# Halving the loads of a 2x upsampling kernel: eight loads with two 8 KiB descriptors per partition in place of four with one of 32 KiB

## The chip, the cores and the metric

The kernel runs on one core of a Trainium2 chip. The metric is the device time of one execution in microseconds (us). The 16 DMA engines of the core move data between DRAM and the on-chip memory SBUF (128 partitions). VectorE (DVE) and ScalarE (ACT) copy inside SBUF. SyncE (SP) only issues DMAs. A *descriptor* is one contiguous piece that one DMA engine moves. Each load or store here is split over all 16 engines, eight partitions each, and each engine works through its pieces in the order in which they were issued. I call that queue of one engine its *ring*.

## The reference

Nearest-neighbour upsampling by 2: each element of x, float32 [16, 64, 64, 64] (16.78 MB), is written to a 2 x 2 square of the output (67.11 MB). No arithmetic is involved.

```python
for i in range(new_h):
    for j in range(new_w):
        result[:, :, i, j] = x[:, :, i // scale_factor, j // scale_factor].copy()
```

## The kernel before

All rows of x are seen as one list of 65,536 rows of 64 numbers (256 bytes). There are four loads (NB = 4) of 4 MiB. Partition p gets 128 consecutive rows: one descriptor of 32 KiB. All four are issued at once, at the start, into buffers of their own. Then, for each of 16 tiles (32 rows per partition), DVE expands rows 0 to 17 and ACT rows 18 to 31 into `u` (32 KiB per partition, two buffers), and SP stores `u` as one 4 MiB DMA.

```python
K, J = 32, 4
NB = R // (P * J * K)
xf = x.rearrange("b c h w -> (b c h) w").rearrange(
    "(n p r) w -> n p r w", n=NB, p=P
)
of = out.rearrange("b c (h hd) w -> (b c h) (hd w)", hd=s).rearrange(
    "(n p r) w -> n p r w", n=NB, p=P
)
KV = 18
xpool = ctx.enter_context(tc.tile_pool(name="xin", bufs=NB))
upool = ctx.enter_context(tc.tile_pool(name="uexp", bufs=2))
xts = []
for n in range(NB):
    xt = xpool.tile([P, J * K, W], fdt, name="xt")
    nc.sync.dma_start(out=xt[:, :, :], in_=xf[n])
    xts.append(xt)
# ... expanded(): a broadcast view that repeats each row and each column twice
for n in range(NB):
    for j in range(J):
        r0 = j * K
        u = upool.tile([P, K, s, W, s], fdt, name="u")
        nc.vector.tensor_copy(out=u[:, :KV], in_=expanded(xts[n][:, r0 : r0 + KV, :]))
        nc.scalar.copy(out=u[:, KV:], in_=expanded(xts[n][:, r0 + KV : r0 + K, :]))
        nc.sync.dma_start(out=of[n, :, r0 : r0 + K, :], in_=u[:, :, :, :, :])
```

(Lines joined; the first load is also moved ahead of the start barrier, which the change leaves alone.)

Of the kernel before, what the change touches and what calls it, by code (L numbers as in the profile page):

```python
# [1 line left out]

# [4 lines left out]


def begin_before_barrier(nc):



    blocks = nc.main_func.blocks
    main, body = blocks[0], blocks[1]
    sp = mybir.EngineType.SP
    load = next(i for i in body.instructions if i.engine == sp)
    assert isinstance(load, mybir.InstDMACopy), type(load)
    assert not (load.sync_info and load.sync_info.on_wait)
    body.instructions = [i for i in body.instructions if i is not load]
    kept = list(main.instructions)  # L20
    at = next(
        n
        for n, i in enumerate(kept)
        if i.engine == sp and isinstance(i, mybir.InstDrain)
    )
    kept.insert(at, load)
    main.instructions = kept


@with_exitstack  # L30
def kernel(
    ctx: ExitStack,
    tc: tile.TileContext,
    x: bass.AP,
    scale_factor: int,
    out: bass.AP,
):
    nc = tc.nc
    nc.at_finalize(begin_before_barrier)
    P = nc.NUM_PARTITIONS  # L40
    s = int(scale_factor)
    B, C, H, W = x.shape
    R = B * C * H
    fdt = x.dtype




    K, J = 32, 4
    NB = R // (P * J * K)  # L50
    assert NB * P * J * K == R
    xf = x.rearrange("b c h w -> (b c h) w").rearrange(
        "(n p r) w -> n p r w", n=NB, p=P
    )
    of = out.rearrange("b c (h hd) w -> (b c h) (hd w)", hd=s).rearrange(
        "(n p r) w -> n p r w", n=NB, p=P
    )

    KV = 18

    xpool = ctx.enter_context(tc.tile_pool(name="xin", bufs=NB))
    upool = ctx.enter_context(tc.tile_pool(name="uexp", bufs=2))

    xts = []
    for n in range(NB):
        xt = xpool.tile([P, J * K, W], fdt, name="xt")
        nc.sync.dma_start(out=xt[:, :, :], in_=xf[n])
        xts.append(xt)

    def expanded(rows):  # L70
        k = rows.shape[1]
        return rows.unsqueeze(2).unsqueeze(4).to_broadcast([P, k, s, W, s])

    for n in range(NB):
        for j in range(J):
            r0 = j * K
            u = upool.tile([P, K, s, W, s], fdt, name="u")
            nc.vector.tensor_copy(  # L78
                out=u[:, :KV], in_=expanded(xts[n][:, r0 : r0 + KV, :])
            )  # L80
            nc.scalar.copy(  # L81
                out=u[:, KV:], in_=expanded(xts[n][:, r0 + KV : r0 + K, :])
            )
            nc.sync.dma_start(
                out=of[n, :, r0 : r0 + K, :], in_=u[:, :, :, :, :]
            )


# [1 line left out]
_INS = ['x', 'scale_factor']  # L90
_OUTS = [((16, 64, 128, 128), 'float32')]

_NUMBERS = {'scale_factor': 2}


# [26 lines left out]
```

## Time and profile before

The time is 199.99 us (median of 3; 199.96 to 200.03).

| what | value | where it is read |
|---|---|---|
| span of the profiled run | 198.2 us | page |
| DMA: bytes, mean rate | 83.89 MB, 423 GB/s | page |
| busy DVE / ACT | 21% / 26% | page |
| one store, steady state | 9.68 us | distance of copies in the timeline |

The page of the kernel before: busy time by engine (us, share of the span, instructions), the DMA row (busy tenths in 40 slices), the packets and the one DMA queue.

```profile
DVE 40.9 (21%) x16; ACT 52.0 (26%) x17; POOL 0.2 (0%) x4
...
DMA  8999999999999999999999999999999999999994
...
DMA packets 2880, 83.89 MB, mean 423 GB/s; under 512 B 320, under 2 KB 320, under 8 KB 320
...
q1 hardware_dynamic: 2880, 83.89, 98.8%
```

The compute engines are idle about three quarters of the time and the DMA engines hardly ever (98.8% busy): the kernel is bound by what they move. There are 2560 data packets and 320 small completion writes.

The timeline of the kernel before (start, duration, engine, line, what, and in brackets the idle time ahead of it and what ended it):

```profile
0.00 2.15 SPq L67 DMA_DIRECT2D xt<-in_x_dram  x4
...
12.35 6.26 ACT L81 COPY u<-xt 128x3584 f32<-128x3584 f32 x2 [10.28 <-DMA xt<-in_x_dram]
...
15.55 165.91 SPq L84 DMA_DIRECT2D out_dram<-u  x16
52.07 3.18 ACT L81 COPY u<-xt 128x3584 f32<-128x3584 f32 x1 [33.47 <-DMA out_dram<-u]
...
61.75 3.18 ACT L81 COPY u<-xt 128x3584 f32<-128x3584 f32 x1 [6.51 <-DMA out_dram<-u]
...
71.43 3.18 ACT L81 COPY u<-xt 128x3584 f32<-128x3584 f32 x1 [6.49 <-DMA out_dram<-u]
```

The third copy of ACT needs the `u` buffer of the first store back, so its start, 52.07, tells when the first store landed. That store was issued near 15.6 us, but it lay behind four loads in the rings. After that a copy starts every 9.68 us: one 4.19 MB store each, 433 GB/s. The 3.2 us copies are hidden, as the other store moves meanwhile.

### The profile page before, as it was taken

The page shows a single profiled execution, that of the slowest core. Times are in us where ns is not written, and L with a number is a line of the kernel's source. Part 1 is how long each engine was busy: PE and PEld are TensorE (multiplying, and loading weights), DVE is VectorE, ACT ScalarE, POOL GpSimd, SP SyncE. Part 2 cuts the span into 40 slices and gives each one's busy share as a digit, 9 for nine tenths or more (in the row PEclk, how much of TensorE's full clock was granted, in tenths as well). Part 3 has the DMA queues.
Part 4 walks back from the last instruction along what each step waited for, and adds up shares of the span by engine and source line. Part 5 has one row for each costly group of instructions (what it writes and reads, how often), then busy time and mean ns, then how long its engine had stood idle before and what let it go on. Part 6 is the DMA issues. An engine that isn't in the chain of part 4 may idle for free.

```text
span 198.2 us, 145 instructions
## 1 busy us (share of the span) xinstructions
DVE 40.9 (21%) x16; ACT 52.0 (26%) x17; POOL 0.2 (0%) x4
## 2 busy tenths in 40 slices
DVE  0055000000405050505050505050505050404000
ACT  2057000000415150606060606060606060505000
POOL 0000000000000000000000000000000000000000
DMA  8999999999999999999999999999999999999994
GB/s 317 423 423 430 450 430 456 370 403 423 423 423 436 436 443 456 436 436 423 423 423 423 423 443 443 450 450 436 423 423 423 423 423 436 436 443 456 436 436 212
DMA packets 2880, 83.89 MB, mean 423 GB/s; under 512 B 320, under 2 KB 320, under 8 KB 320
## 3 DMA queue, kind: packets, MB, share of 16 engines
q1 hardware_dynamic: 2880, 83.89, 98.8%
HBM read 16.78 MB, written 67.11 MB: 423 GB/s over the span
## 4 chain that ended last, share of the span: by engine, by line
DMA 77%; ACT 14%; issue 0%; ACTq 0%
DMA out_dram<-u 70%; ACT u L81 14%; DMA xt<-in_x_dram 6%; ACTq L81 0%
## 5 line engine op out<-in xcount | busy, mean ns | idle before, releaser
L81 ACT COPY u<-xt 128x3584 f32<-128x3584 f32 x16 | 50.8, 3179 | 128.3 <-DMA out_dram<-u 118.0
L78 DVE COPY u<-xt 128x4608 f32<-128x4608 f32 x16 | 40.9, 2560 | 139.6 <-DMA out_dram<-u 127.3
L81 ACT ACT_TABLE_LOAD x1 | 1.3, 1283 | 0.8 <-PEq L103 0.8
L103 POOL MEMSET const-bfloat16-1.0<- 128x1 bf16 x1 | 0.1, 102 | 0.0
L103 POOL MEMSET const-uint8-127<- 128x1 uint8 x1 | 0.1, 102 | 0.0
L103 POOL MEMSET const-float32-0.0<- 128x1 f32 x1 | 0.1, 99 | 0.2 <-issue 0.2
L103 POOL MEMSET const-float32-1.0<- 128x1 f32 x1 | 0.1, 99 | 0.0
## 6 DMA issues: line engine op xcount, KB each, us to landing
out_dram<-u SPq DMA_DIRECT2D x16, 4096.0 KB, 16.1
xt<-in_x_dram SPq DMA_DIRECT2D x4, 4096.0 KB, 25.9
```

Source lines behind the costliest of these rows:

```text
L78: nc.vector.tensor_copy(out=u[:, :KV], in_=expanded(xts[n][:, r0 : r0 + KV, :]))
L81: nc.scalar.copy(out=u[:, KV:], in_=expanded(xts[n][:, r0 + KV : r0 + K, :]))
L103: nc = _bacc.Bacc("TRN2", target_bir_lowering=False, num_devices=1)
```

## The change

The intent is a finer start: a first load of half the size, so that the first tiles can be expanded earlier, while each tile's store becomes one contiguous 4 MiB block of the output.

```diff
-    K, J = 32, 4
-    NB = R // (P * J * K)
-    xf = ... "(n p r) w -> n p r w", n=NB, p=P
-    of = ... "(n p r) w -> n p r w", n=NB, p=P
+    K, J = 32, 2
+    rows = P * K
+    NL = R // (J * rows)
+    xf = x.rearrange("b c h w -> (b c h) w").rearrange(
+        "(n j p k) w -> n p j (k w)", n=NL, j=J, p=P
+    )
+    of = out.rearrange("b c (h hd) w -> (b c h) (hd w)", hd=s)
...
-        xt = xpool.tile([P, J * K, W], fdt, name="xt")
-        nc.sync.dma_start(out=xt[:, :, :], in_=xf[n])
+        xt = xpool.tile([P, J, K, W], fdt, name="xt")
+        nc.sync.dma_start(out=xt[:, :, :, :], in_=xf[n])
...
-            nc.sync.dma_start(
-                out=of[n, :, r0 : r0 + K, :], in_=u[:, :, :, :, :]
-            )
+        nc.sync.dma_start(
+            out=of[t * rows : (t + 1) * rows, :], in_=u[:, :, :, :, :]
+        )
```

(Cut: assertions, pool sizes and the loop over tiles, now `for t in range(NL * J)` with `xt, j = xts[t // J], t % J`.) The loads are now eight of 2 MiB. Per partition each brings two 8 KiB pieces that lie 1 MiB apart in DRAM.

More of the change, by code (lines that the diff above doesn't have):

```diff
@@ L44, with expanded @@
     fdt = x.dtype
-    K, J = 32, 4
-    NB = R // (P * J * K)
-    assert NB * P * J * K == R
+    K, J = 32, 2
+    rows = P * K
+    NL = R // (J * rows)
+    assert NL * J * rows == R
+    KV = 18
     xf = x.rearrange("b c h w -> (b c h) w").rearrange(
-        "(n p r) w -> n p r w", n=NB, p=P
+        "(n j p k) w -> n p j (k w)", n=NL, j=J, p=P
     )
-    of = out.rearrange("b c (h hd) w -> (b c h) (hd w)", hd=s).rearrange(
-        "(n p r) w -> n p r w", n=NB, p=P
-    )
-    KV = 18
-    xpool = ctx.enter_context(tc.tile_pool(name="xin", bufs=NB))
+    of = out.rearrange("b c (h hd) w -> (b c h) (hd w)", hd=s)
+    xpool = ctx.enter_context(tc.tile_pool(name="xin", bufs=NL))
     upool = ctx.enter_context(tc.tile_pool(name="uexp", bufs=2))
     xts = []
-    for n in range(NB):
-        xt = xpool.tile([P, J * K, W], fdt, name="xt")
-        nc.sync.dma_start(out=xt[:, :, :], in_=xf[n])
+    for n in range(NL):
+        xt = xpool.tile([P, J, K, W], fdt, name="xt")
+        nc.sync.dma_start(out=xt[:, :, :, :], in_=xf[n])
         xts.append(xt)
-    def expanded(rows):
-        k = rows.shape[1]
-        return rows.unsqueeze(2).unsqueeze(4).to_broadcast([P, k, s, W, s])
-    for n in range(NB):
-        for j in range(J):
-            r0 = j * K
-            u = upool.tile([P, K, s, W, s], fdt, name="u")
-            nc.vector.tensor_copy(
-                out=u[:, :KV], in_=expanded(xts[n][:, r0 : r0 + KV, :])
-            )
-            nc.scalar.copy(
-                out=u[:, KV:], in_=expanded(xts[n][:, r0 + KV : r0 + K, :])
-            )
-            nc.sync.dma_start(
-                out=of[n, :, r0 : r0 + K, :], in_=u[:, :, :, :, :]
-            )
+    def expanded(part):
+        return part.unsqueeze(2).unsqueeze(4).to_broadcast(
+            [P, part.shape[1], s, W, s]
+        )
+    for t in range(NL * J):
+        xt, j = xts[t // J], t % J
+        u = upool.tile([P, K, s, W, s], fdt, name="u")
+        nc.vector.tensor_copy(out=u[:, :KV], in_=expanded(xt[:, j, :KV, :]))
+        nc.scalar.copy(out=u[:, KV:], in_=expanded(xt[:, j, KV:, :]))
+        nc.sync.dma_start(
+            out=of[t * rows : (t + 1) * rows, :], in_=u[:, :, :, :, :]
+        )
 _INS = ['x', 'scale_factor']
```

## The prediction

> **What bounds the kernel now.** The 16 DMA engines, from start to end. The page's DMA line gives 83.89 MB at a mean of 423 GB/s and one queue that fills 98.8% of the 16 engines' span of 198.2 us; VectorE is busy 21% and ScalarE 26%. The chain of waits is load, then stores; the 3.2 us copies between are hidden by the other buffer's store. In the timeline, copies of the steady state start every 9.68 us (71.43, 81.10, 90.79, ...): one 4.19 MB store per 9.68 us, 433 GB/s. The Trainium skill, "DMA: Bandwidth & Descriptors", section "Where 436 GB/s comes from", gives a ceiling of 435 GB/s for the fabric; this trace is within 1% of it. The trace's completion times: the four loads land at 12.3, 22.0, 31.8 and 42.3 us (9.7 us apart, 10.5 for the last), the first store at 52.0, the others 9.68 us apart.
>
> So about 0.85 us is lost where loads turn into stores.
>
> **What the change does.** Bytes, copies (16 + 16, same shapes), stores (16 x 4 MB) and buffers stay. The first load is half as large, so its data should arrive near 7.5 us instead of 12.3 us, and the first two copies and the first store are issued some 5 us earlier. But all loads are issued in the first 3 to 5 us, ahead of every store, into the same rings: the first store still waits behind 16.78 MB of loads. Gain on the critical path: none. The instruction order also shows that store k of the first eight now waits for load k (shared semaphores); load 1 lands near 12.5 us, still 30 us before the rings run out of loads. No cost.
>
> A store's destination becomes one contiguous 4 MB block instead of 32 KiB pieces 128 KiB apart. Stores already run at 433 GB/s, so I expect nothing there (9.68 us per store stays).
>
> Load descriptors shrink from 32 KiB (32 per engine) to 8 KiB (128 per engine): 96 more per engine, plus 4 more completion writes. The same page, section "Why small descriptors are slow (HBM only)", names a fixed overhead of about 3 cycles per packet: 96 x 3.5 ns = 0.34 us, an estimate. From the trace: 9.68 us / 8 = 1.210 us per 32 KiB descriptor against 1.205 us at the ceiling, so up to 5 ns each, 0.5 us. Alternating between places 1 MiB apart might cost more. I expect the eight loads to land 4.9 us apart, the last near 42.8 us (42.3 before): +0.3 to +1 us, all on the critical path since nothing hides it.
>
> **Prediction:** 200.5 us, 8 in 10 between 199.6 and 202.0. Faster by over 2%: 0.01; within 2%: 0.94; slower by over 2%: 0.05.
>
> **What would show it right or wrong.** Right: first copy starts near 7.5 us; the third copy (first store landed) starts at 52.1 to 53 us, against 52.07; then every 9.68 us; DMA share still near 99%; packets 4480 instead of 2880. Wrong: a store period other than 9.68 us (the contiguous destination matters); loads landing over 5.1 us apart (8 KiB descriptors or the 1 MiB stride cost more); a gap in DMA at 5 to 20 us (the sequencer or the rings can't take eight loads in advance); a different loss where loads turn into stores.
>
> **What would make it wrong.** An 8 KiB read costing 25 ns or more of overhead (96 x 25 = 2.4 us) would put the time above the range. To be 2% faster it would have to beat the 435 GB/s ceiling, which I exclude.

## The result, and the profile after

The time is 199.85 us (median of 4; 199.79 to 199.88), against 200.01 us before (median of 4; 199.96 to 200.46). The ratio is 0.9987, with a 95% interval of 0.9969 to 1.0004: the same within noise. (A ratio here is the mean time of one kernel's fast runs over that of the other's in the same rounds, so not quite the ratio of the medians that I quote.)

The page of the changed kernel, the same lines as before:

```profile
DVE 40.9 (21%) x16; ACT 52.1 (26%) x17; POOL 0.2 (0%) x4
...
DMA  7999999999999999999999999999999999999995
...
DMA packets 4480, 83.89 MB, mean 424 GB/s; under 512 B 384, under 2 KB 384, under 8 KB 384
...
q1 hardware_dynamic: 4480, 83.89, 99.2%
```

The timeline of the changed kernel:

```profile
0.00 13.59 SPq L66 DMA_DIRECT2D xt<-in_x_dram  x8
...
7.67 6.26 ACT L78 COPY u<-xt 128x3584 f32<-128x3584 f32 x2 [5.55 <-DMA xt<-in_x_dram]
...
13.72 167.81 SPq L79 DMA_DIRECT2D out_dram<-u  x16
52.31 3.18 ACT L78 COPY u<-xt 128x3584 f32<-128x3584 f32 x1 [38.38 <-DMA out_dram<-u]
...
61.91 3.18 ACT L78 COPY u<-xt 128x3584 f32<-128x3584 f32 x1 [6.42 <-DMA out_dram<-u]
...
71.57 3.18 ACT L78 COPY u<-xt 128x3584 f32<-128x3584 f32 x1 [6.48 <-DMA out_dram<-u]
```

The first copy starts 4.7 us earlier (7.67 against 12.35), but the first store lands 0.24 us later (52.31 against 52.07). The early start only lengthened ACT's wait for the `u` buffer, from 33.47 to 38.38 us. The eight loads took SP 13.6 us to issue instead of 2 us for four: it was held up, and so the first store was issued only 1.8 us earlier (13.72 against 15.55). That costs nothing here, as the DMA row shows no gap.

The same total hides two differences that nearly cancel. The trace's completion times (16 per DMA, one from each engine; the last is taken) show them. Distances in us:

```
                                   before                 after
loads, 4 MiB each / 2 MiB each     9.70 9.71 10.53        4.96 4.97 4.98 4.97 4.97 4.97 4.96
last load -> first store           9.70                   9.73
stores after that (mean of 15)     9.68                   9.67
```

(1) The changed loads are slower while they run: 2 x 4.97 = 9.94 us per 4 MiB against 9.71. Over four times 4 MiB that is +0.9 us. (2) In the kernel before, the last load takes 0.83 us longer than its fellows; in the changed kernel it does not. I call this the *loss at the turn* from loads to stores. The packets of one engine around it, as the trace records them (start on the trace's own clock, which is 11.05 us ahead of the timeline's before and 11.26 us after; duration, ns). The trace does not name the engine: packets are joined where one starts within a few ns of the end of another.

```
before   49.03 load 1946 | 50.97 load 1653 | 52.63 store 1213 | 53.84 store 1213   (32 KiB each)
after    51.62 load  321 | 51.94 load  309 | ... | 52.87 store 1224 | 54.09 store 1213   (loads 8 KiB)
```

In the kernel before, the last load packet of every engine takes 1.65 to 2.07 us and the one ahead of it up to 1.95 us (1213 ns each until then), and the first store behind them is at full speed at once. The windows view shows the same as rates. Kernel before, its stretch of full-speed loads and the 4 us at the turn (columns: stretch, length, busy DVE, ACT, POOL, clock, DMA share, GB/s; a packet is counted whole where it starts, so short stretches are coarse, as shares over 1 show: 16 packets of 32 KiB more or less are 131 GB/s in 4 us):

```profile
14.00:38.00 24.00, 3.38 (x2) 4.61 (x2) 0.00 (x0) 1.00 1.00 430
38.00:42.00 4.00, 0.00 (x0) 0.00 (x0) 0.00 (x0) 1.00 1.09 377
```

The changed kernel:

```profile
14.00:38.00 24.00, 0.00 (x0) 0.00 (x0) 0.00 (x0) 1.00 1.01 422
38.00:42.00 4.00, 0.00 (x0) 0.00 (x0) 0.00 (x0) 1.00 1.19 500
```

While loads run, 430 against 422 GB/s; at the turn, 377 against 500, which tells the direction but not the size; the landings above give that.

So two questions are left for experiments. Why are the loads slower: descriptor size (theory D, one fixed cost per descriptor), or the places 1 MiB apart (theory A)? And why did the loss at the turn go: descriptor size again (D), the contiguous destination of the stores (theory S), the stores queued behind the loads (theory Q), or is it a fixed price of the loads' end (theory F)?

### The profile page after: what moved, and what is told of

The parts are those of the page before. It is cut to its first block, busy times and chain, and to the rows that moved or that the text cites. A ratio compares the mean times of both kernels' runs of the same rounds, so it can differ in the third digit from the quotient of the medians.

```text
span 198.0 us, 149 instructions
## 1 busy us (share of the span) xinstructions
DVE 40.9 (21%) x16; ACT 52.1 (26%) x17; POOL 0.2 (0%) x4
## 4 chain that ended last, share of the span: by engine, by line
DMA 76%; ACT 14%; issue 0%; ACTq 0%; SPq 0%
DMA out_dram<-u 73%; ACT u L78 14%; DMA xt<-in_x_dram 4%; ACTq L78 0%; SPq L79 0%
```

## The experiments

Twelve kernels ran. Times in us, with the kernel before run on the same chip in the same rounds. "Loss" is how much longer the last load took than the pace of those before it, from completion times.

| run | loads per engine | pace per 4 MiB | loss at the turn | time | ratio to before, 95% |
|---|---|---|---|---|---|
| before | 32 x 32 KiB | 9.71 | 0.83 | 199.99 | |
| changed | 128 x 8 KiB | 9.94 | none | 199.85 | 0.9969 to 1.0004 |
| e1_pad8k | 128 x 8 KiB, adjacent | 9.87 | none | 200.07 | 0.9990 to 1.0017 |
| e2_strided_store | 128 x 8 KiB | 9.94 | none | 200.01 | 0.9986 to 1.0011 |
| e3_one_tile | 128 x 8 KiB, 1 MiB loads | 9.94 | none (0.04) | 199.68 | 0.9972 to 0.9997 |
| e4_taper | 24 x 32, 8 x 24, 8 x 8 KiB | 9.71 | 0.8 | 199.95 | 0.9985 to 1.0010 |
| e5_last_first | 32 x 32 KiB, no store queued | 9.70 | none (0.01) | 204.51 | one run |
| e6_first_store_8k | 32 x 32 KiB | 9.71 | 0.95 | 200.04 | 0.9987 to 1.0018 |
| e7_2k | 512 x 2 KiB | 10.84 | none | 205.01 | one run |
| e8_16k | 64 x 16 KiB | 9.78 | 0.18 | 199.85 | 0.9978 to 1.0003 |
| f1_last_8k | 24 x 32, then 32 x 8 KiB | 9.71, 9.96 | 0.49 | 199.73 | 0.9970 to 0.9995 |
| f2_last_32k | 96 x 8, then 8 x 32 KiB | 9.94 | 0.22 | 199.69 | 0.9963 to 0.9996 |
| f3_gate_half | 24 x 32, 16 x 16 KiB, store late | 9.71 | none | 199.95 | 0.9979 to 1.0006 |
| f4_gate_3_8 | 24 x 32, 8 x 12, 8 x 20 KiB, store late | 9.72 | none | 199.44 | 0.9955 to 0.9980 |

(For f2, the loss is the 9.93 us of its last load less 9.71, the pace of 32 KiB descriptors.) "None" means within 0.05 us of zero or below it. The median of before was 200.04 (e1 to e4), 199.96 (e5 to e8), 200.09 (f1, f3, f4) and 199.94 (f2).

Totals that differ by 0.3 us or less need care. The traces show that the program ends 0.81 to 1.06 us after its last store has landed, and this tail differs between the kernels: 1.06 us in before, e1 and e5, 1.00 in e4, f2, f3 and f4, 0.88 in e6 and f1, 0.81 in the changed kernel, e2, e3, e7 and e8. In the kernel before SP still works through five semaphore waits there, some 0.06 us each, in the changed kernel through one.

### e1_pad8k: only the descriptor size

```diff
 # kernel before
-        xt = xpool.tile([P, J * K, W], fdt, name="xt")
-        nc.sync.dma_start(out=xt[:, :, :], in_=xf[n])
+        xt = xpool.tile([P, J, K * W + 16], fdt, name="xt")
+        nc.sync.dma_start(
+            out=xt[:, :, : K * W],
+            in_=xf[n].rearrange("p (j k) w -> p j (k w)", j=J),
+        )
```

> The kernel before with one thing changed: each SBUF tile is padded by 64 bytes after every 8 KiB, so each of the four loads is made of four 8 KiB descriptors per partition instead of one of 32 KiB, from the same consecutive addresses. Theory D (descriptor size does both things seen): loads land 9.9 us apart instead of 9.7, the extra 0.8 us of the last load goes (under 0.3 us is left), the time is within 0.3 us of the changed kernel (199.85 us). Theory A (the places 1 MiB apart make the loads slower): loads stay 9.7 us apart. Theory S (the contiguous destination of the stores removes the loss at the turn): the last load still lands 10.5 us after the one before it.

The loads landed 9.88, 9.87 and 9.85 us apart: theory D for both differences. Descriptor size alone slows the loads by 0.16 us per 4 MiB and removes the loss, with the stores' addresses untouched. The 0.07 us per 4 MiB that this falls short of the changed kernel's 9.94 may belong to the places apart or to the finer loads; e3 speaks for the latter. The time is not lower because its first load landed 0.56 us later (first copy at 12.91 us against 12.35), together with a longer issue of the four-piece pattern (0.70 against 0.40 us, medians).

### e2_strided_store: only the stores' addresses

```diff
 # changed kernel; wrong output on purpose
-    of = out.rearrange("b c (h hd) w -> (b c h) (hd w)", hd=s)
+    of = out.rearrange("b c (h hd) w -> (b c h) (hd w)", hd=s).rearrange(
+        "(n p q k) w -> n q p (k w)", n=NL * J // 4, p=P, q=4
+    )
-            out=of[t * rows : (t + 1) * rows, :], in_=u[:, :, :, :, :]
+            out=of[t // 4, t % 4], in_=u[:, :, :, :, :]
```

> The changed kernel, with the stores at the addresses of the kernel before (32 KiB pieces 128 KiB apart; the output is wrong on purpose). Theory D: same as the changed kernel within 0.1 us, last load 4.97 us after the one before it. Theory S: the loss of about 0.8 us at the turn from loads to stores comes back, 200.6 us.

Theory S falls: with the old addresses the last load still takes 4.96 us, no loss. The stores average 9.69 us here against 9.67 in the changed kernel: 15 x 0.02 = 0.3 us, too little for these runs to prove. The time is 0.16 us above the changed kernel's, where 0.1 was expected. The Trainium skill, "DMA: Bandwidth & Descriptors", section "Latency and other measured facts", reports slow copies between DRAM tensors at large power-of-two row pitches (2 MiB and up) and close to the full rate at 512 KiB. The pitch here is 128 KiB, and the trace agrees in that it costs nearly nothing (9.69 against 9.67 us per store).

### e3_one_tile: no places 1 MiB apart

```diff
 # changed kernel
-    K, J = 32, 2
+    K, J = 32, 1
```

> The changed kernel with sixteen loads of one tile: still 8 KiB descriptors, but each load reads one contiguous 1 MiB, without places 1 MiB apart. Theory D: 4 MiB of loads take 9.9 us or a little more (twice as many completions), time within 0.2 us of the changed kernel. Theory A: loads return to 9.7 us per 4 MiB, time about 199.0 us.

Sixteen loads land 2.486 us apart on average: 9.94 us per 4 MiB, as in the changed kernel. Theory A falls: contiguous loads are no faster. The time, 199.68, is within the 0.2 us of the changed kernel that theory D gave.

### e7_2k: the cost per descriptor at 2 KiB

```diff
 # changed kernel; wrong output on purpose
-        "(n j p k) w -> n p j (k w)", n=NL, j=J, p=P
+        "(n j p k) w -> n p j (k w)", n=NL, j=4 * J, p=P
...
+            out=xt.rearrange("p j (c k) w -> p (j c) (k w)", c=4), in_=xf[n]
```

> The changed kernel with loads of 2 KiB descriptors (512 per engine instead of 128; wrong output on purpose). A fixed cost per descriptor of 9 ns (from 9.94 against 9.70 us per 4 MiB for 24 descriptors more per engine) gives 0.0835 us each, 42.8 us for all loads, the last landing at about 45.4 us, 203 us in all. [...]

The loads landed 5.42 us apart, 84.7 ns per 2 KiB descriptor: near the 83.5 expected. With it, the average times of four sizes lie on one line. From 2 and 32 KiB: (1213.4 - 84.7) / 30 = 37.6 ns per KiB, and 84.7 - 2 x 37.6 = 9.4 ns fixed.

| descriptor | measured, ns (completion writes included) | 9.4 + 37.6 per KiB |
|---|---|---|
| 32 KiB (before) | 1213.4 | from it |
| 16 KiB (e8) | 611.5 | 611.4 |
| 8 KiB (changed; e1) | 310.5; 308.5 | 310.4 |
| 2 KiB (e7) | 84.7 | from it |

96 descriptors more per engine x 9.4 ns = 0.90 us: the whole of (1).

This cost is an average over a run, and not one constant. Counted packet by packet (16 packets in order of their starts are one per engine), the traces show two stretches. In the changed kernel an engine takes 306.4 ns per 8 KiB descriptor for about its first 40 loads, and 310.6 ns from about 16 us on. The same step comes in e2, e3, f2 and, smaller and later, e1 (306.0, then 308.2); e7 goes from 80 or 81 ns to 84.7 at about 12 us. The early times (1210.1, 608, 306.4 and 81 ns for 32, 16, 8 and 2 KiB) lie close to a line of their own, about 5 ns + 37.65 per KiB; the fixed part roughly doubles later. What doubles it is not shown. Queued stores are not needed for it: in e3 it has come by 18 us, and the first store is issued at 24.84.

The total missed, 205.0 instead of 203: the first load landed at 9.8 us, 4.4 us above its pace of 5.4, where the changed kernel has 2.7 (7.67 less 4.97). One load took SP 5.3 us to issue (median), so here the start and the issue cost too.

### e8_16k: half way

```diff
 # kernel before
-    K, J = 32, 4
+    K, J = 32, 2
```

> The kernel before with eight loads of 2 MiB and one contiguous 16 KiB descriptor per partition. A fixed cost per descriptor: 4 MiB of loads take 9.75 to 9.8 us. The loss at the turn, if it goes with the descriptor size: about 0.4 us; if it is there or not there: 0.8 or 0. Time 199.5 to 200.1 us.

The pace is on the line. The loss is 0.18 us: neither proportional to the descriptor size (0.4) nor there-or-not-there.

### e4_taper: small descriptors only just ahead of the turn

```diff
 # kernel before
-        nc.sync.dma_start(out=xt[:, :, :], in_=xf[n])
+        cut = J * K if n < NB - 1 else (J - 1) * K
+        nc.sync.dma_start(out=xt[:, :cut, :], in_=xf[n, :, :cut, :])
+        if cut < J * K:
+            nc.sync.dma_start(out=xt[:, cut:, :], in_=xf[n, :, cut:, :])
```

> The kernel before with only its last load cut in two: 24 KiB descriptors, then 8 KiB descriptors for the last quarter. Theory D, with the loss at the turn set by the size of the last descriptors before the turn: of 0.83 us some 0.6 us or more goes, little is added (8 descriptors per engine): 199.2 to 199.4 us, faster than both kernels. If the loss is a fixed drain of the read path, or set by the stores: 200.0 us, no change.

This was my idea for a better kernel, and it failed: the last 4 MiB took 7.31 + 3.21 = 10.52 us, the loss as before. The packets show the same slow stretch of about 2.5 us, now over about four of the eight small ones of each engine (one engine: 461, 681, 380 and 596 ns instead of 309). So the loss does not follow the size of the last descriptors.

### e5_last_first: no store behind the loads

```diff
 # kernel before
-    for n in range(NB):
+    for n in reversed(range(NB)):
```

> The kernel before, with the tiles of the last load expanded and stored first, so that no store is queued behind the loads when they end (a bubble of about 6 us comes in between, 206 us). Theory Q (the loss at the turn comes from the queued stores, whose reads start while the last loads are in flight): the last load lands 9.7 us after the one before it, no record of the last two packets over 1.3 us. Theory F (the loss is a property of the end of the loads, whatever follows): 10.5 us again.

The loads landed 9.69, 9.71 and 9.71 us apart, and no packet of the last load took over 1.22 us. Theory F falls and Q holds: the loss comes from the stores that lie queued behind the loads. (The time, 204.51, is below the 206 expected.) The timeline shows that the first store could be issued only at 44.6 us, which leaves the bubble that this kernel pays for.

```profile
41.37 6.26 ACT L81 COPY u<-xt 128x3584 f32<-128x3584 f32 x2 [39.29 <-DMA xt<-in_x_dram]
...
44.58 141.29 SPq L84 DMA_DIRECT2D out_dram<-u  x16
```

### e6_first_store_8k: smaller descriptors behind the turn

```diff
 # kernel before: the first store (n == 0 and j == 0) in parts = 4, others parts = 1
+            k = K // parts
+            for i in range(parts):
+                nc.sync.dma_start(
+                    out=of[n, :, r0 + i * k : r0 + (i + 1) * k, :],
+                    in_=u[:, i * k : (i + 1) * k, :, :, :],
+                )
```

> The kernel before, with the first store cut into four DMAs of 8 KiB descriptors. If the size of the first descriptors behind the loads sets the loss at the turn, the last load lands 9.7 to 9.9 us after the one before it and the time falls by 0.5 us or more (199.3 us). If only what the loads are made of counts, 10.5 us and 200.0 to 200.2 us.

The last load took 10.66 us: what the first store is made of does not matter.

### f1_last_8k and f2_last_32k: does what came earlier count?

```diff
 # f1: kernel before. f2 has `step = K if n < NB - 1 else J * K`
-        nc.sync.dma_start(out=xt[:, :, :], in_=xf[n])
+        step = J * K if n < NB - 1 else K
+        for r in range(0, J * K, step):
+            nc.sync.dma_start(
+                out=xt[:, r : r + step, :], in_=xf[n, :, r : r + step, :]
+            )
```

> The kernel before with its last 4 MiB loaded as four DMAs of 8 KiB descriptors (32 per engine); the first 12 MiB keep 32 KiB descriptors. If the loss at the turn goes once enough of the loads in front of the stores are small, the last load lands 9.95 us after the third, and the time is about 199.4 us. If what came earlier counts (the lead that larger descriptors gained over 12 MiB, about 0.7 us, is given back at the turn), the last load still lands near 42.3 us, 10.5 us after the third, and the time stays 199.9 to 200.0 us.

> The mirror image of the run with the last 4 MiB in small descriptors: the first 12 MiB are loaded as twelve DMAs of 8 KiB descriptors, the last 4 MiB as one load of 32 KiB descriptors. If only the descriptors close to the turn count, the last load takes 10.5 us (loss of 0.8 us) on top of 0.7 us for the small descriptors: 200.7 us. If what came earlier counts as well (a lead that only large descriptors gain and the turn takes back), the last load takes 9.7 to 10.0 us: 199.9 to 200.2 us.

With the last 4 MiB small (f1) the last quarter of it took 2.98 us against 2.49 for the three before: a loss of 0.49. The last load landed at 42.21 us, 10.45 us after the third: close to the second alternative. The time, 199.73, lay between the two, but 0.18 us of it is the shorter tail; the last store landed at 197.16 us, as in the kernel before (197.15). With the first 12 MiB small and the last 4 MiB large (f2) the loss is only 0.22 us, although large descriptors stand right at the turn: 11 packets on the 16 engines are slow (1.3 to 1.9 us). Its time, 199.69, is below both ranges expected. The descriptors 4 to 16 MiB away count more than those at the turn. Ordered by descriptors per engine, the losses are 0.83 (32), 0.8 (40), 0.49 (56), 0.18 (64), 0.22 (104), none (128, 512): the more descriptors have gone before, the smaller the loss.

### f3_gate_half and f4_gate_3_8: the first store held back

The last load is cut in two; the tile in its first part is stored first, so the first store cannot be issued before that part has landed.

```diff
 # f4: kernel before. f3 has `J * K // 2`
+        cut = J * K if n < NB - 1 else J * K * 3 // 8
+        nc.sync.dma_start(out=xt[:, :cut, :], in_=xf[n, :, :cut, :])
+        if cut < J * K:
+            nc.sync.dma_start(out=xt[:, cut:, :], in_=xf[n, :, cut:, :])
...
+    order = [(n, j) for n in range(NB) for j in range(J)]
+    order.remove((NB - 1, 0))
+    order.insert(0, (NB - 1, 0))
+    for n, j in order:
```

> The kernel before with its last load cut in two halves, and a tile of the first half stored first, so that the first store is issued at about 39.9 us (half lands at 36.6 us, copies 3.2 us) instead of 15.6 us. Theory Q (queued stores take from the loads in flight in the last 3 us): most of the loss of 0.83 us goes, but up to 0.5 us of bubble may come, as the loads leave the engines at about 40.6 us: 199.2 to 199.8 us. If stores queued or not is nothing to the loss: 200.0 us or more, the last load 10.5 us after the third.

> As the run before, with the cut at three eighths: the first store is issued at about 38.6 us. Theory Q: the loads in flight are disturbed for less than with stores queued early, and no bubble comes: loss between 0 and 0.83 us, 199.2 to 199.9 us. If the moment of issue does not matter as long as it is before the loads' end: 200.0 us.

The timeline of f4:

```profile
35.49 6.26 ACT L87 COPY u<-xt 128x3584 f32<-128x3584 f32 x2 [33.44 <-DMA xt<-in_x_dram]
...
38.70 142.16 SPq L90 DMA_DIRECT2D out_dram<-u  x16
51.34 3.18 ACT L87 COPY u<-xt 128x3584 f32<-128x3584 f32 x1 [9.59 <-DMA out_dram<-u]
```

Its rates at the turn, to be set against the 377 GB/s of the kernel before:

```profile
38.00:42.00 4.00, 2.52 (x2) 3.75 (x2) 0.00 (x0) 1.00 1.12 480
```

The first store is issued at 38.7 us instead of 15.55 and lands *earlier*: 51.34 against 52.07 us. The first two copies start 23 us later, and yet 0.73 us are gained, as the loads in front are left alone. This is theory Q a second time, in a kernel with a correct result. The cut is not the reason: e4 cuts its last load in two as well, with the stores issued early, and keeps its loss. Nor is a store behind the loads enough: f4's is in the rings 2.9 us before the last load lands (41.58 us) and does no harm. It has to be there earlier. f4 is 0.33% faster than the kernel before (199.44 us) and has the lowest median of all; it was not run in the same rounds as the changed kernel (199.85 us). The gain is real but below the 2% that would be called a difference.

f3 frees its first `u` buffer at 51.34 us too, but keeps nothing of it, and its time, 199.95, misses the 199.2 to 199.8 that theory Q gave: its stores then come every 9.73 us instead of 9.68 (15 x 0.05 = 0.75 us). f4's stores average 9.69, with 9.72 to 9.74 for most of the last eight. What makes stores slower in these kernels (and in e5, 9.73) I did not find: their packets take 1219 ns on average in e5 and f3 and 1215 in f4 instead of 1213.

## Why the prediction was right or wrong

- *The DMA engines bound the kernel; an earlier first copy gains nothing.* Right. The first copy came at 7.67 us (expected near 7.5) and ended up as waiting time. The loads were not issued in 3 to 5 us as forecast but in 13.6, without cost.
- *Loads +0.3 to +1 us.* Right, at its upper end: 9.94 against 9.71 us per 4 MiB is +0.9 us. The term was sized from the 3 cycles per packet (3.5 ns, an estimate) of the Trainium skill, "DMA: Bandwidth & Descriptors", section "Why small descriptors are slow (HBM only)", and from 5 ns per descriptor read off the stores. The traces show about 5 ns for the first 40 or so, but 9.4 ns on average. The 1 MiB distance adds nothing that the runs can see (e3).
- *Stores unchanged, 9.68 us.* Right: 9.67 us; e2 puts the destination's effect at some 0.02 us per store.
- *About 0.85 us is lost where loads turn into stores* was taken as a fixed part of both kernels. This is the step that failed. The loss is 0.83 us with 32 descriptors per engine and none with 128. The prediction named "a different loss where loads turn into stores" as a sign of being wrong, and that is what came. The middle of the forecast, 200.5 us, was 0.65 us too high, mainly for this reason, and inside its range. That the time came out equal to the kernel before is a cancellation that the prediction did not foresee; with the loss kept, it would have been some 0.8 us longer and still in the range.
- The sum, from the landings: +0.16 us at the last load (+0.29 for the first 4 MiB, +0.70 for the other three, less the 0.83 of the turn), +0.19 at the first store, +0.08 at the last store (197.23 against 197.15). In these two traces the changed kernel thus moves its data no faster at all. Its tail after that is 0.25 us shorter (0.81 against 1.06), which makes -0.17, against a measured -0.16 us between the medians. The small gain, inside the noise as it is, lies in the end of the program.

What is shown of the loss at the turn: it needs stores that lie in the rings behind the loads early enough (e5, f3 and f4 have none of it), it shrinks, though not in step, with the number of load descriptors that went before (e1, e8, f1, f2), and it does not depend on the stores' addresses (e2) or the first store's descriptors (e6). It also goes with the two stretches of e7's section: kernels whose loads took the slower pace long before the turn (changed, e1, e2, e3, e7) have none, and the kernel before, whose loads never did, has it whole; e8 and f1, which took it late, lie between, but so does f2, which took it early. That is a correlation that no run tested. Why is only argued. The Trainium skill, "DMA: Bandwidth & Descriptors", section "Two DMAs through the same engine are not ordered", says that the read and write sides of an engine are separate queues. A read side that runs ahead would start on the stores while the last loads are still in flight, and take from them; if each descriptor's fixed cost falls on the read side, many small descriptors would eat up that lead. The slow stretch fits this: about 3.7 us before the first store in the kernel before, 2 us in f1, 1.3 to 1.9 us in f2, absent in the changed kernel. No run here sees the two sides apart, so this stays open; e8's 0.18 us with 64 descriptors, lower than f2's 0.22 with 104, is not explained by a count alone.

## What to carry to other kernels

When the DMA engines are busy from end to end, making data arrive earlier only lengthens a wait; cost the change by descriptors (here 5 ns each at first and 9.4 on average) and look for places where the rate falls, such as the turn from loads to stores. A loss that one kernel shows at such a place is not a constant: before carrying it over into a forecast, ask what in the kernel makes it. And before a difference of a few tenths of a us is put down to the change, look where in the run it arises: here it lay behind the last store. Queueing work as early as possible is not always free either: here, issuing the first store 23 us later made it land 0.73 us earlier.

## What the Trainium skill lacked or had wrong

- "DMA: Bandwidth & Descriptors", section "Why small descriptors are slow (HBM only)": about 3 cycles per packet (3.5 ns, an estimate at the 850 MHz of the section "Where 436 GB/s comes from"). The descriptors here cost about 5 ns at first, near that figure: 306.4 ns per 8 KiB load, and 306.5 for the 8 KiB stores of e6. The page has no word of the later stretch, where a load costs 310.6 ns, or 9.4 ns of fixed cost on average.
- The same page says nothing of a loss where queued stores follow loads: up to 0.83 us (0.95 in e6), with the last load packet of each engine at 1.65 to 2.07 us instead of 1.21 per 32 KiB, gone when the first store is issued only 1.7 to 2.9 us before the last load lands (f3, f4).
- The same page does not say how many descriptors the rings take before the issuing engine is held up. Here SP issued four loads of 8 descriptors per engine in 2.15 us, but eight loads of 16 took 13.6 us, and one store's issue was then held up for 8.7 us.
- No page has a reason for the store pace of 9.73 us instead of 9.68 that e5 and f3 show once the first store starts late.
